# Another order of preparing v's tiles, five tiles of u ahead, and gathering that ends sooner, in a two-block kernel

## The chip, the cores and the metric

The kernel runs on one core of one Trainium2 chip. The metric is the device time of one execution in microseconds (us), as a median of runs. Five engines work side by side, each through its own instructions in the written order: TensorE (matrix products, with weight loads shown apart as PEld), VectorE (DVE), ScalarE (ACT), GpSimd (POOL, which here issues the indirect gathers) and SyncE (SP, which issues the other DMAs). Semaphores order them against each other.

## The reference

Two transformer blocks, one after the other, on 512 tokens of width 1024 in float32. Each block mixes tokens (the first by pooling and retention over a context, the second by HGRN2 and S5) and then runs a PEER layer: a product-key lookup chooses 16 of 16,384 experts for each token and each of 8 heads, and

    act = gelu(u[eidx] . h)            # one number per chosen expert
    out = sum(gate * act * v[eidx])    # rows of v, width 1024

where `u` and `v` are tables of 16,384 rows of 1024 numbers. The change touches only this PEER layer, which runs twice.

## The kernel before

Tokens come in four groups of 128. For three groups (`ND` = 3, 384 tokens, `TD`) the PEER layer is computed **densely**: all 16,384 experts are gone through in 128 tiles of 128 experts. A *tile of u* gives gelu(u.h) of 128 experts for 384 tokens; multiplied with a table of gates G (zero where an expert isn't chosen) this becomes the weights of a *tile of v*, whose products add up in six PSUM banks (`pv`). For the fourth group the chosen rows are **gathered** by indirect DMAs, 128 of u and 128 of v, 512 KB each, and are worked on by VectorE, one instruction per row (`sparse`, lines 2280, 2296, 2301). Each float32 operand is split into a high part in fp32r and the rest (`split`, lines 108 to 114), and each product is three matmuls (`mm3`, lines 118 to 120).

The first `L0` = 60 tiles of u are done earlier, while the gates are being computed, and their activations are parked in DRAM (*old* tiles, `Go` and `old` are their gates and activations, loaded four tiles at a time). The remaining 68 are done in `steady`, together with all 128 tiles of v and the gathering. `steady` is where the change lies:

- `LEAD` tiles of u are done first, with the loads of v's first two tiles issued after the first of them; then the first tile of v is prepared.
- A loop of 124 passes follows. Pass i issues the loads of v's tile i+2 on SP, does a tile of u where the schedule `s_by` asks for one (none after pass `S_END` = 112), calls `side`, prepares v's tile i+1 (`v_prep`) and issues the matmuls of v's tile i. Tiles of u call `side` once more. Tiles 124 to 127 of v are prepared on the way in other buffers and multiplied at the end.
- `side` owes gathered rows at a steady pace: 256/`full` rows per call, times `VF` after pass 112. When all 256 are consumed, it goes on with the finishing steps of the fourth group (`done`, `take`, `update`, `squares`, `factor`, lines 2312 to 2366), one per call; the first of them loads a row of gates from DRAM and uses it in the same call.
- `order` says which tile of v comes in which pass: a new one if its activation was made long enough ago, an old one otherwise.

`v_prep` turns a loaded tile of v (`raw`, named `vr`) into `vh` and `vl`, multiplies the activations with the gates (line 2255, in place), and splits the product into `wh` and `wl`. ScalarE writes the high parts, VectorE the rest. A tile of v can be multiplied once `wh` and `vh` are there; `vl` and `wl` are needed by the second and third matmul of a group. `vh`, `vl`, `wh`, `wl` have two buffers, `vr` three, a gathered row five, the gelu'd activation of a new tile six. A tile of u has one PSUM bank (`p0`), so the next tile of u waits until gelu has read it. Nothing is reordered by a scheduler: each engine works in the order in which the Python code issues.

Of the kernel before, what the change touches and what calls it, by code (L numbers as in the profile page):

```python
# [10 lines left out]
F32 = mybir.dt.float32  # L11
# [4 lines left out]
AF = mybir.ActivationFunctionType  # L16
ALU = mybir.AluOpType
# [11 lines left out]
class Env:  # L29
# [6 lines left out]
    def __init__(self, tc):  # L36
        self.tc, self.nc = tc, tc.nc
        self.now = 0
        self.queue = []
        self.chains = []  # L40
        self.fill, self.rate, self.owed = None, 0.0, 0.0
# [66 lines left out]
def split(nc, src, hi, lo, e_hi="act", e_lo="dve"):  # L108

    if e_hi == "act":  # L110
        nc.scalar.activation(hi, src, AF.Copy)  # L111
    else:
        (nc.vector if e_hi == "dve" else nc.gpsimd).tensor_copy(hi, src)
    (nc.vector if e_lo == "dve" else nc.gpsimd).tensor_tensor(lo, src, hi.bitcast(F32), op=ALU.subtract)  # L114
# [1611 lines left out]
class Peer:  # L1726
# [5 lines left out]
    LAG = 4  # L1732
    NQ, NT = 42, 8
    L0 = 60
    LEAD = 2
    S_END = 112
    RATE, RATE_T = 1.3, 1.3
    QT = 2
    WLO = "dve"
    SPARSE_END = 122  # L1740
    VF = 0.5

    def __init__(self, E, pfx, wq, key_rows, u, uT, v, AB, done, fill):
        self.E, self.pfx = E, pfx
        self.tc, self.nc = E.tc, E.nc
        self.wq, self.key_rows, self.u, self.uT, self.v = wq, key_rows, u, uT, v
        self.AB, self.done, self.fill, self.after = AB, done, fill, None
        self.TD = self.ND * 128
        self.few = sum(r.shape[1] for r in key_rows) <= 8
        self.U, self.V, self.Gt, self.act_tiles, self.old = {}, {}, {}, {}, {}  # L1750

        n = 128 - self.L0
        self.s_by = [min(n, self.LEAD + (i + 1) * (n - self.LEAD) // self.S_END) for i in range(128)]
        self.order, new, old = [], self.L0, 0
        for i in range(128):
            have = self.s_by[i - 1 - self.LEAD] if i > self.LEAD else 0
            if old == self.L0 or (new - self.L0 < have and i < 124):
                self.order.append(new)
                new += 1
            else:  # L1760
                self.order.append(old)
                old += 1
        assert sorted(self.order) == list(range(128)) and self.order[124] // self.GE == self.order[127] // self.GE
# [344 lines left out]
    def steady(self, vp, psv):  # L2108
# [5 lines left out]
        done = 0  # L2114
        for _ in range(self.LEAD):
            self.s_step(self.L0 + done)
# [7 lines left out]
        owed = 0.0  # L2124
        full = self.s_by[-1] - self.LEAD + self.S_END + self.VF * (self.SPARSE_END - self.S_END)
        finish = None
# [21 lines left out]
        def side():  # L2148
            nonlocal owed
            owed += 256 / full * (1.0 if i < self.S_END else self.VF)  # L2150
            while owed >= 1 and finish is None:
# [87 lines left out]
    def v_prep(self, e, vp, spare=False):  # L2239
        if e >= 128:  # L2240
            return
        nc = self.nc
        raw, G = self.V[e]
        if spare:
            vh, vl = (self.sp.tile([128, 8, 128], F32R, name=n).rearrange("p a b -> p (a b)") for n in ("uh", "ul"))
            p, n, b = (self.fp, "hs", 1) if e == 124 else (self.sp, "ur", 3)
            w2 = p.tile([128, 1024], F32R, name=n, bufs=b)
            wh, wl = (w2[:, i * self.TD:(i + 1) * self.TD] for i in range(2))
        else:
            vh, vl = (vp.tile([128, 1024], F32R, name=n, bufs=2) for n in ("vh", "vl"))  # L2250
            wh, wl = (vp.tile([128, self.TD], F32R, name=n, bufs=2) for n in ("wh", "wl"))
        split(nc, raw, vh, vl, "act", "dve")
        act = self.act_tiles.pop(self.order[e])
        a3 = act.rearrange("p (c t) -> p c t", t=self.TB)
        nc.vector.tensor_tensor(a3, a3, G, op=ALU.mult)  # L2255
        split(nc, act, wh, wl)
        self.V[e] = (wh, wl, vh, vl)

    def v_mm(self, es):
# [170 lines left out]
```

## Time and profile before

| | |
|---|---|
| median of 3 runs | 3644.05 us (3637.18 to 3645.54) |
| profiled execution, its own time | 3638.08 us |
| its span on the core | 3636.3 us |
| mean granted TensorE clock | 0.973 |
| TensorE busy | 3406.6 us (94%) |
| VectorE busy | 2829.1 us (78%) |
| ScalarE busy | 1380.6 us (38%) |
| GpSimd busy | 1117.7 us (31%) |
| DMA | 830.20 MB, mean 228 GB/s |

`steady` runs from about 1108 to 1962 us in the first block and from about 2771 to 3628 us in the second. A row of a timeline gives the start and the duration in us, the engine, the line, the operation, what it writes and reads, and in brackets how long the engine stood idle before and what ended that. PEld rows tell best when TensorE starts on something, since ends of matmuls are modelled.

### The profile page before, as it was taken

To read this page: it belongs to the slowest core of one execution; us is meant where nothing else is said; L and a number is where in the kernel's file an instruction comes from. 1 tells how busy PE (TensorE), PEld (TensorE's weight loads), DVE (VectorE), ACT (ScalarE), POOL (GpSimd) and SP (SyncE) were. 2 spreads that over 40 slices of the span, in tenths; PEclk is the share of its full clock that TensorE was granted. 3 is DMA by queue.
4 is the path that set the end of the run, shared out by engine and by line. 5 is a ranking of instruction groups with operands and counts; after the bars stand their busy time and mean duration, and the time that the engine had idled before them with its cause. 6 is when DMAs were issued, how large, how long until landed. Compare 5 with 4: busy or idle time off the path is not lost. (4 is left out here: it accounts for less than half of the span.)

```text
span 3636.3 us, 50853 instructions
## 1 busy us (share of the span) xinstructions
PE 3406.6 (94%) x18339; PEld 2992.4 (82%) x18339; DVE 2829.1 (78%) x6079; ACT 1380.6 (38%) x1930; POOL 1117.7 (31%) x1076
## 2 busy tenths in 40 slices
PE   8989887999998999999998888999998999999998
PEld 5878676999887888888886778899887888888886
DVE  6654743898996888888877685788996888888886
ACT  4223333332673333333334324432574333333333
POOL 3212675000003444444431432000001445444451
PEclk9999998999999999999998989999999999999999
DMA  5442754443459999999993213244457999999995
GB/s 189 137 148 71 217 172 104 131 135 126 176 201 327 359 345 352 339 338 348 329 322 115 70 57 103 95 141 139 143 206 269 341 373 325 350 341 336 348 323 193
DMA packets 418747, 830.20 MB, mean 228 GB/s; under 512 B 37948, under 2 KB 249776, under 8 KB 415424
## 3 DMA queue, kind: packets, MB, share of 16 engines
q1 hardware_dynamic: 344320, 558.41, 45.3%
q0 software_dynamic: 74176, 268.55, 20.3%
q8 instruction: 144, 2.36, 0.3%
q14 instruction: 107, 0.88, 0.1%
HBM read 744.52 MB, written 82.33 MB: 227 GB/s over the span
## 5 line engine op out<-in xcount | busy, mean ns | idle before, releaser
L2280 POOL DMA_INDIRECT gr<-in_peer_u_dram,rb x256 | 367.9, 1437 | 1406.5 <-DMA ur<-in_peer_u_tiles_dram 491.1
L118 PE MATMUL pv<-vh,wh 128*128 128x512 f32 x1512 | 602.3, 398 | 48.6 <-ACT wh L111 48.1
L120 PE MATMUL pv<-vh,wl 128*128 128x512 f32 x1512 | 604.3, 400 | 0.0
L119 PE MATMUL pv<-vl,wh 128*128 128x512 f32 x1512 | 594.6, 393 | 0.0
L2280 POOL DMA_INDIRECT gr<-in_peer_v_dram,rb x256 | 371.6, 1452 | 405.3 <-DVE accs L2301 343.0
L114 DVE TENSOR_TENSOR ul<-ur,uh 128x1024 fp32r<-128x1024 f32 x260 | 318.0, 1223 | 128.2 <-ACT uh L111 126.5
L118 PEld LDWEIGHTS pv<-vh,wh 128*128 128x128 f32 x1512 | 286.5, 189 | 126.7 <-ACT wh L111 75.2
L114 DVE TENSOR_TENSOR vl<-vr,vh 128x1024 fp32r<-128x1024 f32 x252 | 308.1, 1223 | 79.2 <-ACT vh L111 77.3
L118 PE MATMUL p<-hi,uh 128*128 128x384 f32 x1088 | 365.6, 336 | 1.4 <-ACT act L2074 1.4
L120 PE MATMUL p<-hi,ul 128*128 128x384 f32 x1088 | 365.7, 336 | 0.3 <-DVE ul L114 0.3
L119 PE MATMUL p<-lo,uh 128*128 128x384 f32 x1088 | 365.3, 336 | 0.0
L120 PEld LDWEIGHTS pv<-vh,wl 128*128 128x128 f32 x1512 | 286.1, 189 | 86.8 <-DVE wl L114 29.3
L118 PE MATMUL mm<-hi,uh 128*128 128x384 f32 x960 | 333.9, 348 | 3.6 <-ACT qT L1832 3.6
L119 PEld LDWEIGHTS pv<-vl,wh 128*128 128x128 f32 x1512 | 286.9, 190 | 52.6
L2301 DVE SCALAR_TENSOR_TENSOR accs<-gr,rb,accs 128x1024 f32<-128x1024 f32 x254 | 325.7, 1282 | 5.5 <-DMA gr<-in_peer_v_dram,rb 0.7
L120 PE MATMUL mm<-hi,ul 128*128 128x384 f32 x960 | 324.2, 338 | 4.5 <-DVE ul L114 4.5
L119 PE MATMUL mm<-lo,uh 128*128 128x384 f32 x960 | 323.0, 337 | 0.0
L2296 DVE SCALAR_TENSOR_TENSOR gr<-gr,hs 128x1024 f32<-128x1024 f32 x256 | 303.2, 1219 | 0.0
L111 ACT ACTIVATE vh<-vr 128x1024 fp32r<-128x1024 f32 x252 | 265.9, 1055 | 60.1 <-PE pv L120 30.8
L111 ACT ACTIVATE uh<-ur 128x1024 fp32r<-128x1024 f32 x260 | 272.6, 1048 | 5.5 <-DMA ur<-in_peer_u_tiles_dram 5.5
L118 PE MATMUL mm<-hi,whi 128*128 128x512 f32 (+1 forms) x656 | 262.3, 400 | 1.1 <-ACT hi L311 1.1
L120 PE MATMUL mm<-hi,wlo 128*128 128x512 f32 (+1 forms) x656 | 252.7, 385 | 1.3 <-DVE wlo L114 1.3
(625 smaller groups left out, 7079.5 us busy)
## 6 DMA issues: line engine op xcount, KB each, us to landing
ur<-in_peer_u_tiles_dram SPq DMA_DIRECT2D x256, 512.0 KB
vr<-in_peer_v_dram SPq DMA_DIRECT2D x252, 512.0 KB
raw<-in_w_in_dram SPq DMA_DIRECT2D x60, 512.0 KB
ada<-in_ada_w_dram SPq DMA_DIRECT2D x96, 256.0 KB
fG<-gst SPq DMA_DIRECT2D x12, 2048.0 KB
f_2G<-gst SPq DMA_DIRECT2D x12, 2048.0 KB
x<-in_ada_w_dram SPq DMA_DIRECT2D x64, 256.0 KB
raw<-in_peer_wq_dram SPq DMA_DIRECT2D x32, 512.0 KB
```

The costliest lines, as they stand in the source:

```text
L111: nc.scalar.activation(hi, src, AF.Copy)
L114: (nc.vector if e_lo == "dve" else nc.gpsimd).tensor_tensor(lo, src, hi.bitcast(F32), op=ALU.subtract)
L118: nc.tensor.matmul(out, a_hi, b_hi, start=start, stop=False)
L119: nc.tensor.matmul(out, a_hi, b_lo, start=False, stop=False)
L120: nc.tensor.matmul(out, a_lo, b_hi, start=False, stop=stop)
L2280: nc.gpsimd.indirect_dma_start(out=r, out_offset=None, in_=self.u if n < 128 else self.v, in_offset=bass.IndirectOffsetOnAxis(ap=self.eidx ...
L2296: nc.vector.scalar_tensor_tensor(r, r, 1.0, self.hs, op0=ALU.mult, op1=ALU.mult, accum_out=dots[:, j:j + 1])
L2301: nc.vector.scalar_tensor_tensor(accs, r, w[:, j:j + 1], accs, op0=ALU.mult, op1=ALU.add)
```

## The change

`v_prep` issues its five instructions in another order: the product with the gates first, then both high parts on ScalarE, then both low parts on VectorE. `LEAD` goes from 2 to 5; what `order` used of `LEAD` (how long ago an activation must have been made) becomes a constant of its own, `WAIT` = 2, the value it had. `SPARSE_END`, the pass by which the pace of gathering is set, goes from 122 to 118, and `VF` from 0.5 to 0.6.

```diff
-    LEAD = 2
+    LEAD = 5
+    WAIT = 2
...
-    SPARSE_END = 122
-    VF = 0.5
+    SPARSE_END = 118
+    VF = 0.6
...
-            have = self.s_by[i - 1 - self.LEAD] if i > self.LEAD else 0
+            have = self.s_by[i - 1 - self.WAIT] if i > self.WAIT else 0
...
-        split(nc, raw, vh, vl, "act", "dve")
         act = self.act_tiles.pop(self.order[e])
         a3 = act.rearrange("p (c t) -> p c t", t=self.TB)
         nc.vector.tensor_tensor(a3, a3, G, op=ALU.mult)
-        split(nc, act, wh, wl)
+        nc.scalar.activation(vh, raw, AF.Copy)
+        nc.scalar.activation(wh, act, AF.Copy)
+        nc.vector.tensor_tensor(vl, raw, vh.bitcast(F32), op=ALU.subtract)
+        nc.vector.tensor_tensor(wl, act, wh.bitcast(F32), op=ALU.subtract)
```

## Rows read from the trace of the kernel before

**Rows 1.** Page, busy us of each engine, share of the span, instructions.
```profile
PE 3406.6 (94%) x18339; PEld 2992.4 (82%) x18339; DVE 2829.1 (78%) x6079; ACT 1380.6 (38%) x1930; POOL 1117.7 (31%) x1076
```
**Rows 2.** Stretches: us, busy of PE, PEld, DVE, ACT, POOL; clock, DMA share, GB/s.
```profile
1120.00:1125.00 5.00, 0.00 (x0) 0.00 (x0) 0.00 (x0) 0.29 (x1) 0.00 (x0) 0.52 1.02 405
...
1500.00:1600.00 100.00, 98.67 (x478) 85.54 (x477) 84.62 (x95) 34.26 (x47) 49.11 (x34) 1.00 0.95 341
...
2900.00:3000.00 100.00, 97.28 (x468) 83.59 (x467) 84.16 (x125) 34.11 (x46) 47.81 (x32) 1.00 0.99 363
```
**Rows 3.** Timeline of PEld, block one: first weight load of a tile each.
```profile
1389.77 0.19 PEld L118 LDWEIGHTS p<-hi,uh 128*128 128x128 f32 x1
...
1393.98 0.19 PEld L118 LDWEIGHTS pv<-vh,wh 128*128 128x128 f32 x1
...
1398.02 0.19 PEld L118 LDWEIGHTS p<-hi,uh 128*128 128x128 f32 x1
...
1519.85 0.19 PEld L118 LDWEIGHTS pv<-vh,wh 128*128 128x128 f32 x1 [0.20 <-ACT wh L111]
...
1886.70 0.19 PEld L118 LDWEIGHTS pv<-vh,wh 128*128 128x128 f32 x1
...
1890.78 0.19 PEld L118 LDWEIGHTS pv<-vh,wh 128*128 128x128 f32 x1
```
**Rows 4.** Waits of PEld, 1135 to 1885 us: total us, times, longest.
```profile
PEld pv L118 <- ACT wh L111: 16.4, 43, 1.3
```
**Rows 5.** Timeline of DVE and ACT ahead of the load at 1519.85.
```profile
1516.40 1.05 ACT L111 ACTIVATE vh<-vr 128x1024 fp32r<-128x1024 f32 x1
...
1517.49 1.23 DVE L114 TENSOR_TENSOR vl<-vr,vh 128x1024 fp32r<-128x1024 f32 x1 [0.63 <-ACT vh L111]
...
1518.63 0.55 DVE L2255 TENSOR_TENSOR act<-act,Gn 128x384 f32<-128x384 f32 x1
...
1519.27 0.53 ACT L111 ACTIVATE wh<-act 128x384 fp32r<-128x384 f32 x1 [1.82 <-DVE act L2255]
...
1519.83 0.56 DVE L114 TENSOR_TENSOR wl<-act,wh 128x384 fp32r<-128x384 f32 x1 [0.65 <-ACT wh L111]
```
**Rows 6.** Timeline of PEld, start of `steady` in block one.
```profile
1108.74 0.19 PEld L118 LDWEIGHTS p<-hi,uh 128*128 128x128 f32 x1
...
1113.82 0.19 PEld L118 LDWEIGHTS p<-hi,uh 128*128 128x128 f32 x1 [0.90 <-ACT act L2074]
...
1128.10 0.29 PEld L118 LDWEIGHTS pv<-vh,wh 128*128 128x128 f32 x1 [10.17 <-ACT wh L111]
...
1134.79 0.19 PEld L118 LDWEIGHTS p<-hi,uh 128*128 128x128 f32 x1
```
**Rows 7.** Timeline of PEld, block two: start of `steady`, and v's tile 113.
```profile
2776.88 0.19 PEld L118 LDWEIGHTS p<-hi,uh 128*128 128x128 f32 x1 [1.14 <-ACT act L2074]
...
2794.56 0.29 PEld L118 LDWEIGHTS pv<-vh,wh 128*128 128x128 f32 x1 [13.03 <-ACT wh L111]
...
2800.89 0.19 PEld L118 LDWEIGHTS p<-hi,uh 128*128 128x128 f32 x1
...
3553.93 0.19 PEld L118 LDWEIGHTS pv<-vh,wh 128*128 128x128 f32 x1
```
**Rows 8.** Timeline of ACT: the first tile of v in either block.
```profile
1124.71 1.06 ACT L111 ACTIVATE vh<-vr 128x1024 fp32r<-128x1024 f32 x1 [5.93 <-DMA vr<-in_peer_v_dram]
...
2791.17 1.06 ACT L111 ACTIVATE vh<-vr 128x1024 fp32r<-128x1024 f32 x1 [8.79 <-DMA vr<-in_peer_v_dram]
```
**Rows 9.** Ends of the stages: DVE, ACT, PEld timelines; tile `pv`, first and last start.
```profile
1911.02 0.56 DVE L114 TENSOR_TENSOR wl<-old,wh 128x384 fp32r<-128x384 f32 x1 [0.65 <-ACT wh L111]
...
1924.48 1.06 ACT L111 ACTIVATE vh<-vr 128x1024 fp32r<-128x1024 f32 x1 [2.31 <-DMA vr<-in_peer_v_dram]
...
1962.20 0.13 PEld L272 LDWEIGHTS p<-ident,frr 128*128 128x128 f32 x1
...
L120 PE MATMUL pv<-vh,wl x1512: 387/389/683, 1129.1 to 3627.6; 128*128 128x512 f32 x189
```

## The prediction

> **What bounds the kernel now.** I read the busy times first: TensorE is busy 94% of the span [rows 1]. So an edit on another engine pays only where TensorE waits for it. The change touches the two stretches in which `steady` runs, 1108 to 1962 and 2771 to 3628 us. There TensorE runs at full clock, VectorE is busy some 85 us of 100, and DMA carries 341 to 363 GB/s [rows 2]. A busy share doesn't show lost matmul time, because a matmul's end is modelled; the starts of the weight loads do. So I read the timeline of those next. A tile of u takes 1393.98 - 1389.77 = 4.21 us; a tile of v takes 4.04 us before a tile of u and 4.08 us before another tile of v [rows 3]. Whatever exceeds this is waiting, and it falls into three places.
>
> *The middle of each stage.* From 1134.79 (second weight-load group of u after the first tile of v, [rows 6]) to 1886.70 [rows 3] there are 66 tiles of u and 112 of v; 46 of these are followed by another v. Unhindered: 66 x 4.21 + 66 x 4.04 + 46 x 4.08 = 732.2 us, and 1.9 us for two short transposes of the filler. Measured 751.9, so 17.8 us are lost. In stage two, 2800.89 to 3553.93 [rows 7] is 753.0: 18.9 us lost. The waits name the cause: TensorE for `wh` of ScalarE, 43 times, up to 1.3 us [rows 4]. I then read one such wait on the other engines [rows 5]: `vh` starts at 1516.40 and `wh` ends at 1519.80, 3.4 us later, though the two conversions together take 1.6 us. ScalarE stands still, because `wh` needs the gated product, and that product is queued on VectorE behind `vl`, which itself needs `vh`. When no tile of u lies between two tiles of v, this chain and the free-buffer wait in front of it fill the 4.08 us of the running tile and some more (0.20 us here [rows 3]).
>
> *The start of each stage.* Two tiles of u, then TensorE waits 10.17 and 13.03 us for the first `wh` [rows 6, 7], because ScalarE has waited until 1124.71 and 2791.17 for the first tile of v to arrive [rows 8], with DMA at 405 GB/s [rows 2]. The first tile of v then takes 6.69 us, at a granted clock of about half.
>
> *The end of each stage.* From the start of v's tile 113, fifteen tiles unhindered are 61.2 us. They take 1962.20 - 1886.70 = 75.5 and 3627.6 - 3553.93 = 73.7 us [rows 3, 7, 9]: 14.3 and 12.5 us lost.
>
> **The change part by part.**
>
> *New order in `v_prep`.* Nothing is added: the same five instructions for each of the 256 tiles. The product goes to the front on VectorE, where it waits for nothing of ScalarE; `wh` follows `vh` directly. From the start of `vh`, `wh` is ready after 1.05 + 0.53 = 1.6 us instead of 3.4, `vl` after 1.05 + 1.23 = 2.3, `wl` after 2.8 (durations [rows 5]). The tightest case has `vh` start 0.35 us after the tile before last has left its buffer, so the first matmul's operands are there 2 us before TensorE wants them, and `vl` and `wl` 1.4 and 1 us before. VectorE also loses its stall ahead of `wl` (0.65 us here). A wait of up to 1.3 us fits into this slack. I take 90% of 17.8 + 18.9: **33 us** gained. Bounds: all of it, 36.7; and 15, if the denser gathering puts VectorE late as often as not.
>
> *Denser gathering.* `LEAD` and `VF` change the step of the pacing: `full` was 66 + 112 + 0.5 x 10 = 183 and becomes 63 + 112 + 0.6 x 6 = 178.6, so a call of `side` owes 256/178.6 = 1.433 rows instead of 1.399. A loop pass makes 1 + 63/112 calls instead of 1 + 66/112: 2.24 rows against 2.22. Almost no more work per pass, but the pass shrinks from 751.9/112 = 6.71 us to 4.04 + 0.02 + 0.5625 x 4.21 = 6.43. VectorE's 85% of the stretch [rows 2] includes operations of the same kinds; per pass it grows by 4% of itself at most, and stays under 90%. I cost it at nothing; its cover is the 2 us of slack above.
>
> *Five tiles of u first.* The three extra tiles leave the passes (12.6 us a stage) and go into the idle start. They share one PSUM bank, so each waits for its gelu: spacing 1113.82 - 1108.74 = 5.08 us [rows 6]. In stage one the fifth starts at 1129.1 if its load is there. That load stands on SP's queue behind v's first two tiles; the first arrived by 1124.71, the two 0.52 MB transfers behind it take 2.6 us at 405 GB/s, so 1127.3, plus 1.05 for `uh`: in time. It ends at 1133.3; gelu, `vh` and `wh` (0.5 + 1.05 + 0.5 and hand-overs, 2.3 us) put the first tile of v at 1135.6. It ends at 1139.7 at full clock, 1142.3 at the half clock it had; before it ended at 1134.79. Gain: 12.6 less 4.9 to 7.5; I take 6.5. In stage two the load arrives at 2791.2 + 2.6 = 2793.8, so the fifth tile starts at 2794.9, ends at 2799.1 to 2801.7; v ends at 2805.5 to 2810 instead of 2800.89. Gain 12.6 less 4.6 to 9: I take 5.5. Together **12 us**, bounds 0 (the load a further 6 us late in each stage, since later loads of u now wait for buffers ahead of v's third tile) and 20 (all idle time filled).
>
> *`SPARSE_END` 118.* Counting the owed rows, gathering finishes at pass 119 instead of 123. The last additions leave passes 119 to 122, but the finishing steps move up. In VectorE's order the first `take` and `update` now stand in pass 119 **ahead** of the preparation of v's tile 120, and they need the gate row, whose DMA SP issues behind the gates and activations of v's last group (which wait for `wl` of tile 119) and v's tiles 124 and 125. Before, the next load at that place was v's: `wl` of 119 ended at 1911.58, that load was there at 1924.48 [rows 9], 12.9 us. So VectorE stops for some 13 us, plus 1.4 for the gain row behind it, plus 2 until the next `wh`, in all 16 us from the end of `wl`; TensorE has one or two finished tiles (4 to 8 us) and waits 8 to 12 us, and 2.6 for the clock. Against that, the 14.3 and 12.5 us lost there now shrink: the preparations are shorter by 1.8 us each, and the finishing steps no longer stand behind the last preparation. I set the end of the stages at **0**, bounds 10 gained and 15 lost, for both stages together.
>
> **The sum.** 33 + 12 + 0 = 45 us. The profiled execution took 3638.08 us (span 3636.3), 6 under the median of 3644.05 of the runs shown, which lie from 3637.18 to 3645.54. 3638 - 45 = 3593, and 3599 counted from the median; I forecast 3596.
>
> **The rivals.**
>
> *DMA becomes the bound: slower.* A pass moves 0.52 MB for v, 0.29 for u, 1.17 for 2.24 gathered rows, 0.28 for gates and old activations: 2.27 MB. At 6.43 us that is 353 GB/s. For it: DMA is already 95 to 99% busy at 341 and 363 GB/s [rows 2]. Against it: the same queues carried 405 GB/s at the start [rows 2], and in the middle of a stage almost no wait ends on a DMA. If DMA sustains only the 340 GB/s of today's pass (2.28 MB in 6.71 us), the pass stays at 6.7 us, nothing is gained in the middle, and v's first tile ends later by 6 and 7 us: 3638 + 13 = 3651. It decides below 341 GB/s, where a pass lasts 6.66 us and the lost start is just paid.
>
> The Trainium skill, in "DMA: Bandwidth & Descriptors" (Where 436 GB/s comes from), says that transfers between HBM and SBUF are bound by a core's share of HBM, about 358 GB/s. By that figure a pass would need 6.34 us (an estimate), just under 6.43, with nothing left for the filler's loads in the first third; the trace's 405 GB/s disagrees with it as a ceiling, and I lower this rival's chance accordingly.
>
> *The waits only change their name.* TensorE waits for `vl` or `wl` instead of `wh`, since three rows gathered one after the other hold VectorE up in front of the preparation. Then half of the middle's gain comes and half the start's: 3638 - 16.5 - 6 = 3615, or 3618 between profile and median.
>
> *The finishing steps cost.* The stop on the gate row isn't paid by shorter preparations: 12 us lost in each stage, 3596 + 24 = 3620.
>
> *The order does nothing*, because ScalarE's conversions weren't what is late: against it stand 43 waits of its name [rows 4]. Under 2%, counted with the DMA rival's milder form.
>
> **How the numbers follow.** Forecast 0.66 (3580 to 3612 as its own range), waits renamed 0.15, finishing steps 0.11, DMA bound 0.08. Ranging from 3578 (nearly all waits gone, and the end gains) to 3630 leaves out DMA bound and the outer ends of the others. About 0.2%, 7 us, is what a measurement can tell from no change. Faster: 0.66 + 0.15 + 0.11 less a little for overlaps, 0.89; same 0.04; slower 0.07, all from DMA.
>
> **What would show it.** Right: between v's first tile and tile 113 the weight loads of v following v start 4.08 us apart, and TensorE's waits for `wh` in the middle fall from 16 us to a few; five tiles of u 5.1 us apart, then a gap near 2.5 us; on VectorE a stop of 8 us or more in front of the first `take`, with the gate row's DMA as its releaser. Wrong: waits in the middle that end on DMAs of `vr`, `ur` or `gr`; the fifth u tile starting after 2800 us, or the like in stage one; ends of stages that lose over 25 us each.

## The result and the profile after

The changed kernel takes 3596.59 us (median of 4 runs, 3594.71 to 3598.08) against 3641.76 us before (4 runs, 3637.18 to 3645.54): ratio 0.9876, 95% interval 0.9863 to 0.9888, so 45 us faster. The forecast was 3596 us. The total is right, but in part by luck: the start gave half of what was forecast, and the middle and the ends gave more, as the experiments show.

The profiled execution took 3594.71 us, with a span of 3592.6 us and a mean granted clock of 0.974. The busy times of the page answer to [rows 1]: TensorE's share stays at 94%, and the span is shorter.

```profile
PE 3379.7 (94%) x18339; PEld 3007.1 (84%) x18339; DVE 2806.9 (78%) x6079; ACT 1359.8 (38%) x1930; POOL 1055.7 (29%) x1076
```

The stretches (columns as in [rows 2]) show TensorE busy all the time in the middle of either stage, VectorE 87 to 88 us of 100, and DMA at 357 to 364 GB/s with a share of 0.99 to 1.00; the first row is the start of block one, at half clock.

```profile
1130.00:1135.00 5.00, 3.75 (x11) 3.37 (x12) 2.92 (x3) 2.15 (x3) 0.00 (x0) 0.50 0.39 112
...
1500.00:1600.00 100.00, 100.00 (x493) 89.17 (x492) 87.44 (x97) 33.63 (x48) 49.07 (x35) 1.00 1.00 357
2900.00:3000.00 100.00, 100.00 (x486) 87.77 (x485) 88.39 (x132) 34.92 (x49) 45.83 (x34) 1.00 0.99 364
```

**The middle.** TensorE's waits between 1150 and 1860 us have no row at all. Before, there were 43 waits for `wh` [rows 4] and, in the row behind them in the same view, 46 for `wl` (total us, times, longest):

```profile
PEld pv L120 <- DVE wl L114: 13.6, 46, 0.3
```

In block two, 2800 to 3510 us, the longest entry is this one. It stood there before as well, behind 15.1 us of waits for `wh`:

```profile
PEld pv L118 <- ACT act L2075: 1.7, 2, 0.9
```

The timeline of PEld (first weight load of a tile each) answers to [rows 3], with no idle time in front of any: a tile of u takes 4.21 us, a tile of v 4.04 behind a tile of u and 4.08 behind another tile of v. Behind it, the timeline of DVE and ACT shows a preparation in the new order, as [rows 5] does the old: the product ends before `vh` begins, `wh` follows `vh` at once, and `wl` is done 2.8 us after the start of `vh`.

```profile
1389.51 0.19 PEld L118 LDWEIGHTS p<-hi,uh 128*128 128x128 f32 x1
...
1393.72 0.19 PEld L118 LDWEIGHTS pv<-vh,wh 128*128 128x128 f32 x1
...
1397.76 0.19 PEld L118 LDWEIGHTS p<-hi,uh 128*128 128x128 f32 x1
...
1401.98 0.19 PEld L118 LDWEIGHTS pv<-vh,wh 128*128 128x128 f32 x1
...
1406.02 0.19 PEld L118 LDWEIGHTS pv<-vh,wh 128*128 128x128 f32 x1
...
1410.10 0.19 PEld L118 LDWEIGHTS p<-hi,uh 128*128 128x128 f32 x1
...
1516.68 0.55 DVE L2255 TENSOR_TENSOR act<-act,Gn 128x384 f32<-128x384 f32 x1
1517.91 1.05 ACT L2256 ACTIVATE vh<-vr 128x1024 fp32r<-128x1024 f32 x1
1518.86 0.52 ACT L2257 ACTIVATE wh<-act 128x384 fp32r<-128x384 f32 x1
1518.99 1.23 DVE L2258 TENSOR_TENSOR vl<-vr,vh 128x1024 fp32r<-128x1024 f32 x1 [1.76 <-ACT vh L2256]
1520.13 0.55 DVE L2259 TENSOR_TENSOR wl<-act,wh 128x384 fp32r<-128x384 f32 x1
```

**The start.** Timeline of PEld, ACT and SP in block one, against [rows 6]. Three tiles of u follow the first at 5.0 to 5.1 us each, but TensorE waits 4.26 us for the fifth, which then lasts 6.6 us instead of 4.2, at the granted clock of 0.50 shown above. ScalarE had waited 6.94 us for its load, which SP issued behind v's two; the conversion of that load stands on ScalarE in front of the fourth tile's gelu, which frees the PSUM bank.

```profile
1107.78 0.19 PEld L118 LDWEIGHTS p<-hi,uh 128*128 128x128 f32 x1
...
1122.88 0.19 PEld L118 LDWEIGHTS p<-hi,uh 128*128 128x128 f32 x1 [0.90 <-ACT act L2075]
1131.25 0.28 PEld L118 LDWEIGHTS p<-hi,uh 128*128 128x128 f32 x1 [4.26 <-ACT act L2075]
1140.15 0.19 PEld L118 LDWEIGHTS pv<-vh,wh 128*128 128x128 f32 x1 [2.25 <-ACT wh L2257]
...
1145.02 0.19 PEld L118 LDWEIGHTS p<-hi,uh 128*128 128x128 f32 x1
...
1129.77 1.06 ACT L111 ACTIVATE uh<-ur 128x1024 fp32r<-128x1024 f32 x1 [6.94 <-DMA ur<-in_peer_u_tiles_dram]
...
1111.08 1.73 SPq L2237 DMA_DIRECT2D vr<-in_peer_v_dram  x2
1112.91 7.47 SPq L2058 DMA_DIRECT2D ur<-in_peer_u_tiles_dram  x3
```

**The end.** Timeline of DVE, PEld and SP at v's tile 120 in both blocks; before, nothing like it stood there [rows 9]. VectorE's first `take` waits 14.15 and 8.27 us for the gate row, whose load SP issued only at 1895.45 in block one, and TensorE waits behind it.

```profile
1904.51 0.69 DVE L2330 TENSOR_TENSOR vr<-accs,gr 128x512 f32<-128x512 f32 x1 [14.15 <-DMA gr<-gate]
...
3544.35 0.69 DVE L2330 TENSOR_TENSOR vr<-accs,gr 128x512 f32<-128x512 f32 x1 [8.27 <-DMA gr<-gate]
...
1907.78 0.29 PEld L118 LDWEIGHTS pv<-vh,wh 128*128 128x128 f32 x1 [12.55 <-ACT wh L2257]
...
3547.62 0.29 PEld L118 LDWEIGHTS pv<-vh,wh 128*128 128x128 f32 x1 [6.67 <-ACT wh L2257]
...
1891.89 3.25 SPq L2237 DMA_DIRECT2D ur<-in_peer_v_dram  x2
1895.45 0.40 SPq L2318 DMA_DIRECT2D gr<-gate  x1
```

Every profile is reduced in the same way to what TensorE loses in the three places, in us, block one / block two. *Start*: from the first tile of u to the end of v's first tile, less 4.21 for each tile of u in front. *Middle*: what the stretch up to v's tile 113 takes over its tiles at 4.21, 4.04 and 4.08 and over 1.9 us for the filler's operations. *End*: from tile 113 to the last weight load, over 61.2. Each row is one profiled execution; the median beside it is of 4 to 11 runs. On the chips of the experiments the kernel before had medians of 3641.7 to 3644.8 us; every ratio below is to the kernel before on the same chip. The two kernels and all that was tried:

| kernel | start | middle | end | median us |
|---|---|---|---|---|
| before | 17.6 / 20.9 | 17.8 / 18.9 | 14.3 / 12.5 | 3641.8 |
| changed | 16.2 / 16.2 | 0.1 / 0.6 | 15.2 / 10.3 | 3596.6 |
| 1 order alone | 18.9 / 18.9 | 0.2 / 2.7 | 6.9 / 2.1 | 3587.7 |
| 2 five tiles alone | 19.2 / 19.3 | 19.7 / 20.1 | 16.2 / 12.7 | 3640.5 |
| 3 pace alone | 20.6 / 20.5 | 24.4 / 22.3 | 26.4 / 25.1 | 3666.1 |
| 4 changed, steps held back | 15.6 / 17.5 | 0.1 / 0.6 | 11.8 / 5.4 | 3587.0 |
| 5 changed, steps and row loads held back | 16.2 / 17.0 | 0.1 / 0.6 | 7.7 / 3.5 | 3581.5 |
| 6 changed, old pace | 16.3 / 16.4 | 0.1 / 0.6 | 5.7 / 0.9 | 3579.3 |
| 7 as 6, four tiles | 14.0 / 14.3 | 0.1 / 0.6 | 6.8 / 2.1 | 3578.7 |
| 8 as 6, v's loads later | 12.2 / 12.3 | 0.1 / 0.7 | 5.6 / 1.0 | 3573.6 |
| 9 as 8, v prepared ahead | 7.2 / 7.6 | 0.1 / 0.6 | 5.5 / 1.0 | 3560.4 |
| 10 as 9, weights in pass 123 | 7.2 / 7.2 | 0.1 / 0.6 | 7.8 / 1.0 | 3563.9 |
| 11 as 9, weights after the passes | 7.2 / 7.5 | 0.1 / 0.6 | 0.9 / 0.9 | 3558.6 |

Between before and changed the table gives 6.1 at the start, 36.0 in the middle and 1.3 at the end, 43.4 of the 43.7 us between the two spans. Outside these stretches executions differ by a few us: the profiled ones of 3 and 9 lie 5 and 6.5 us above their medians.

### The profile page after: what moved, and what is told of

The parts are those of the page before. It is cut to its first block, busy times and chain, and to the rows that moved or that the text cites. A ratio compares the mean times of both kernels' runs of the same rounds, so it can differ in the third digit from the quotient of the medians.

```text
span 3592.6 us, 50851 instructions
## 1 busy us (share of the span) xinstructions
PE 3379.7 (94%) x18339; PEld 3007.1 (84%) x18339; DVE 2806.9 (78%) x6079; ACT 1359.8 (38%) x1930; POOL 1055.7 (29%) x1076
## 4 chain that ended last, share of the span: by engine, by line
PE 72%; DVE 16%; POOL 3%; DMA 3%; issue 3%; ACT 2%; SPq 1%; DVEq 0%; ACTq 0%; POOLq 0%
PE pv L118 9%; PE pv L119 9%; PE pv L120 9%; PE mm L118 8%; PE mm L119 8%; PE mm L120 8%; DVE ga L2036 5%; PE p L118 5%; PE p L120 5%; PE p L119 5%; DVE gb L2032 3%; DMA ada<-in_ada_w_dram 1%; DVE ul L114 1%; DMA ur<-in_peer_u_tiles_dram 1%; PE ch L1913 1%
## 5 line engine op out<-in xcount | busy, mean ns | idle before, releaser
L2283 POOL DMA_INDIRECT gr<-in_peer_u_dram,rb x256 | 336.0, 1313 | 1419.9 <-DMA ur<-in_peer_u_tiles_dram 979.3
L118 PE MATMUL pv<-vh,wh 128*128 128x512 f32 x1512 | 591.4, 391 | 22.8 <-ACT wh L2257 22.8
L120 PE MATMUL pv<-vh,wl 128*128 128x512 f32 x1512 | 590.7, 391 | 0.0
L2283 POOL DMA_INDIRECT gr<-in_peer_v_dram,rb x256 | 343.6, 1342 | 390.9 <-DVE accs L2304 331.4
L118 PEld LDWEIGHTS pv<-vh,wh 128*128 128x128 f32 x1512 | 285.0, 188 | 81.5 <-ACT wh L2257 25.1
L2075 ACT ACTIVATE act<-p 128x384 f32<-128x384 f32 x136 | 66.9, 492 | 702.3 <-PE p L120 691.4
```

The source lines that it names most:

```text
L118: nc.tensor.matmul(out, a_hi, b_hi, start=start, stop=False)
L120: nc.tensor.matmul(out, a_lo, b_hi, start=False, stop=stop)
L2283: nc.gpsimd.indirect_dma_start(out=r, out_offset=None, in_=self.u if n < 128 else self.v, in_offset=bass.IndirectOffsetOnAxis(ap=self.eidx ...
```

## The experiments

**The three parts alone (1 to 3).** Each takes one hunk of the diff and leaves the others.

```diff
 order alone: v_prep as changed; LEAD, SPARSE_END, VF as before
 five tiles alone
-    LEAD = 2
+    LEAD = 5
+    WAIT = 2
...
-            have = self.s_by[i - 1 - self.LEAD] if i > self.LEAD else 0
+            have = self.s_by[i - 1 - self.WAIT] if i > self.WAIT else 0
 pace alone
-    SPARSE_END = 122
-    VF = 0.5
+    SPARSE_END = 118
+    VF = 0.6
```

> Only the new order in v_prep; LEAD 2, SPARSE_END 122 and VF 0.5 as before. My theory (the product queued behind vl is what makes wh late): TensorE's waits in the middle of both stages go, 17.8 + 18.9 us; the starts stay as they were; the ends keep their late finishing steps and lose 3 to 5 us less each. 3642 - 37 - 8 = 3597, between 3590 and 3605, so about as fast as the whole change. Rival (order and five tiles ahead only work together, since prepared tiles need activations made earlier): 3615 to 3630, with waits for wh left in the middle.

> Only LEAD 5 (WAIT 2), old order in v_prep, old pace. From the trace of the changed kernel the start gains 1.4 and 4.7 us. With the old order the passes without a tile of u are 49 instead of 46 per stage, each losing about 0.4 us: 2.4 us back. My theory: 3642 - 6 + 2 = 3638, between 3632 and 3643. Rival (what I forecast, 12 us at the start): 3630.

> Only SPARSE_END 118 and VF 0.6, old order, LEAD 2. My theory: the finishing steps come four passes earlier, VectorE stops on the gate row in front of the preparation of v's tile 120 (14.2 and 8.3 us in the changed kernel), and the old, longer preparations follow: slower by 4 to 14 us, 3646 to 3656. Rival (gathering that ends sooner frees VectorE and DMA for the end of the stage): faster by 3 us or more, under 3639.

Against 3642.1 us of before on the same chip: order alone 3587.74 us (ratio 0.9855, 0.9839 to 0.9870); five tiles alone 3640.52 (0.9997, 0.9988 to 1.0006); pace alone 3666.06 (1.0063, 1.0049 to 1.0077). The second is in its range; the first is faster than its range and the third slower. The order alone gains 54 us, more than the whole change, because it also takes 17.8 us out of the ends (14.3 to 6.9 and 12.5 to 2.1; the longest tile there goes from 9.1 to 6.2 us). Of TensorE's waits between 1150 and 1860 us one is left (total, times, longest):

```profile
PEld pv L120 <- DVE wl L2258: 0.3, 1, 0.3
```

The pace alone costs 24 us between the medians; the table shows most of its loss at the ends, where VectorE's stop on the gate row has the same form as in the changed kernel. Timeline of DVE, pace alone:

```profile
1934.90 0.69 DVE L2327 TENSOR_TENSOR vr<-accs,gr 128x512 f32<-128x512 f32 x1 [12.83 <-DMA gr<-gate]
...
3609.16 0.69 DVE L2327 TENSOR_TENSOR vr<-accs,gr 128x512 f32<-128x512 f32 x1 [10.13 <-DMA gr<-gate]
```

The five tiles alone gain nothing. TensorE's waits of 1150 to 1860 us stay as they were without the new order (first line: total, times, longest; compare [rows 4]), and the two starts lose 38.5 us together, exactly as before. In the old order the wait for v's first `wh`, behind the fifth tile of u, is 4.12 us (second line, timeline of PEld) instead of the 2.25 of the changed kernel:

```profile
PEld pv L118 <- ACT wh L111: 18.0, 45, 1.7
...
1143.26 0.19 PEld L118 LDWEIGHTS pv<-vh,wh 128*128 128x128 f32 x1 [4.12 <-ACT wh L111]
```

**What in the pace costs (4 to 6).** First the finishing steps are kept out of the passes before 122; then the loads of gate row and gain row as well; then the old pace is put back.

```diff
 4: in side()
-            if finish is not None:
+            if finish is not None and i >= self.HOLD:    # HOLD = 122
 5: in ending(), ahead of self.done(rows)
             yield from sps
+            while i < 122:
+                yield
 6:
-    SPARSE_END = 118
-    VF = 0.6
+    SPARSE_END = 122
+    VF = 0.5
```

> The changed kernel, but the finishing steps (take and what follows) begin in pass 122 at the earliest; gathering and the load of the gate row stay in pass 119. My theory: the stop on the gate row no longer stands in front of tile 120, the waits of 12.6 and 6.7 us and the slow clock behind them (1.7 and 2.5 us) go, some of it comes back as later finishing work: 3597 - 16 = 3581, between 3574 and 3588. Rival (in block one tile 120 itself comes late, behind 2 MB of preloaded weights, in both cases it is the load that TensorE waits for): 3591 to 3597, the wait only changing its releaser to the load of v.

> The changed kernel with the old pace of gathering (SPARSE_END 122, VF 0.5): the new order and the five tiles of u stay. Theory: the denser pace is what costs in the changed kernel (the stop on the gate row ahead of tile 120's preparation, late loads of v behind it); without it the end of the stages loses 7 and 2 us as with the order alone, and the start keeps the changed kernel's 16.2 us in each block against 18.9 with the order alone: 3587.7 - 2 x 2.7 = 3582 us (3577 to 3587). Rival: the five tiles of u cost what the pace seemed to cost (they shift the schedule of tiles of u, and with it the pass in which gathering ends): 3592 us or more.

> The changed kernel with its dense pace, but the whole of the finishing part, the loads of its gate row and gain row included, not before pass 122 (before, with only the steps held back and the two loads left in pass 119, the ends still lost 11.8 and 5.4 us). Theory: denser gathering itself costs nothing; its price is the finishing part moved up, half as VectorE's stop on the gate row, half because the two row loads stand on SP's queue in front of v's last tiles. Then the ends lose 5.7 and 0.9 us as with the old pace, and the time is that of the old pace, 3579 us (3575 to 3584). Rival: the denser gathering delays v's last tiles by itself (transfers collide): 3587 us as with the steps alone held back.

4 took 3587.04 us (ratio to before 0.9844, 0.9831 to 0.9858), inside the theory's range but at its slow end, and the rival's sign is there too. The stop on the gate row is gone, but SP still issues the two rows in pass 119, in front of v's last tiles, and ScalarE now waits for those, 8.40 us at the longest (in 6 the same wait is 4.63). Timeline of ACT and SP of 4, block one:

```profile
1910.91 1.06 ACT L2257 ACTIVATE vh<-vr 128x1024 fp32r<-128x1024 f32 x1 [8.40 <-DMA vr<-in_peer_v_dram]
...
1899.21 0.40 SPq L2319 DMA_DIRECT2D gr<-gate  x1
1899.66 0.42 SPq L2320 DMA_DIRECT2D lo<-in_final_g_dram  x1
1900.12 3.26 SPq L2238 DMA_DIRECT2D vr<-in_peer_v_dram  x3
```

6 took 3579.26 us (0.9829, 0.9815 to 0.9844), as the theory said: 17 us less than the changed kernel. Its ends lose 5.7 and 0.9 us instead of 15.2 and 10.3, and its middle exactly what the changed kernel's does. 5 took 3581.54 us (0.9824, 0.9810 to 0.9838), in its range: with the dense pace kept and the whole finishing part moved back, all but 4.6 us of the 18.9 that the pace adds at the ends is gone. So denser gathering by itself is nearly free; what it moves up isn't.

**What in the five tiles falls short (7 to 9).** All with the old pace.

```diff
 7:
-    LEAD = 5
+    LEAD = 4
 8 and 9, in steady():
-            if not done:
+            if done == 1:
                 self.v_load(0, vp)
                 self.v_load(1, vp)
 9 also: v_prep(0, vp) ahead of the last s_step, not behind it
         for _ in range(self.LEAD):
+            if done == self.LEAD - 1:
+                self.v_prep(0, vp)
             self.s_step(self.L0 + done)
```

> As the run with the old pace, but four tiles of u in front (LEAD 4) instead of five: those whose loads have landed when the stage begins. Theory: the fourth ends 19.4 us after the first began, wh is there 2.3 us later if v's first tile has landed (some 16 us after the first tile of u began in the kernel before), and v's first tile ends after 25.8 to 28.4 us: less 4 x 4.21 a start of 9 to 11.5 us instead of 16.2, so 3582 - 12 = 3570 us (3565 to 3576). Rival: the loads of u's next tiles in front of v's third, or v's first tile landing late, eat it: 3578 us or more.

> As the run with the old pace, and the loads of v's first two tiles are issued after the second tile of u, behind the load of u's fifth tile, no longer in front of it. Theory: the fifth tile of u stops for 4.3 us and then runs at half clock only because its load lands behind v's; with the load in front, it starts 5.1 us after the fourth, at full clock, and the start loses some 11 us in each block instead of 16.2: 3582 - 10 = 3572 us (3566 to 3577), with no wait of ScalarE for u's fifth tile. Rival: DMA carries all it can there, so v's first tile lands later by as much and TensorE stops in front of it: no difference to the run with the old pace, within 3 us.

> As the run with the old pace and the loads of v behind that of u's fifth tile, and v's first tile is prepared ahead of the fifth tile of u instead of behind it. Theory: the 2.8 us that TensorE still waits for v's first wh, and the slow clock in the tile behind it (6.2 to 6.5 us instead of 4.04), are the preparation's own chain, which the fifth tile of u hides when v's first tile has landed by then: the start loses some 8 us in each block instead of 12.2, so 3573.6 - 8 = 3565 us (3561 to 3570). Rival: v's first tile lands too late for that, VectorE and ScalarE stop in front of it and hold up the gelu or the next tile of u: 3573 us or more.

7 took 3578.67 us (0.9824, 0.9811 to 0.9838): no better than five tiles, against the theory. The starts lose 4.4 us less than those of 6, not some 12, and the ends 2.3 more. The same load of u is still in the way. The fifth tile's `uh` stands in front of the fourth tile's gelu and v's `vh` on ScalarE and waits for its load until 1127.20; TensorE stands 5.89 us. Timeline of ACT and PEld of 7:

```profile
1127.20 1.06 ACT L111 ACTIVATE uh<-ur 128x1024 fp32r<-128x1024 f32 x1 [6.66 <-DMA ur<-in_peer_u_tiles_dram]
...
1128.53 1.05 ACT L2256 ACTIVATE vh<-vr 128x1024 fp32r<-128x1024 f32 x1
...
1130.59 0.29 PEld L118 LDWEIGHTS pv<-vh,wh 128*128 128x128 f32 x1 [5.89 <-ACT wh L2257]
```

8 took 3573.56 us (0.9812, 0.9798 to 0.9825), 5.7 less than 6, in the range of the theory. The fifth tile starts 5.0 us after the fourth and runs at full clock; v's first tile still waits 2.82 us and takes 6.19. Timeline of PEld of 8:

```profile
1129.09 0.19 PEld L118 LDWEIGHTS p<-hi,uh 128*128 128x128 f32 x1 [0.90 <-ACT act L2075]
...
1136.03 0.19 PEld L118 LDWEIGHTS pv<-vh,wh 128*128 128x128 f32 x1 [2.82 <-ACT wh L2257]
...
1142.22 0.19 PEld L118 LDWEIGHTS p<-hi,uh 128*128 128x128 f32 x1
```

9 took 3560.43 us (0.9764, 0.9751 to 0.9777), a little under its range: v's tile lands at 1132.7, is ready before u's fifth tile ends, and takes 4.04 us with no wait. Of the 13 us between the medians of 8 and 9 the table shows 9.7 in the starts; where the rest lies is not shown. Timeline of ACT and PEld of 9:

```profile
1132.72 1.06 ACT L2257 ACTIVATE vh<-vr 128x1024 fp32r<-128x1024 f32 x1 [1.36 <-DMA vr<-in_peer_v_dram]
...
1131.41 0.19 PEld L118 LDWEIGHTS p<-hi,uh 128*128 128x128 f32 x1 [0.90 <-ACT act L2075]
...
1135.51 0.19 PEld L118 LDWEIGHTS pv<-vh,wh 128*128 128x128 f32 x1
...
1139.55 0.19 PEld L118 LDWEIGHTS p<-hi,uh 128*128 128x128 f32 x1
```

**What is left at the end of block one (10 and 11).** With the old pace block one still loses 5.6 us and block two 1. Only block one loads 2 MB of the next stage's weights in pass 117.

```diff
             if i == 117 and self.after is not None:
                 self.after.preload()
 10: the same two lines at i == 123, behind v's loads
 11: behind the loop over the passes and v_prep(127)
```

> As the run before it, and the 2 MB of the next stage's weights that SP issues in pass 117 of block one are issued in pass 123. Theory: block one's end loses 5.6 us and block two's 1.0 with the same order of work, because these 2 MB stand in front of v's tiles 119 to 122 in block one; without them the end of block one loses 1 to 2 us: 4 us less than the run before it, 3561 us (3557 to 3566). Rival: the loss is the late load of the old activations behind a busy queue, or the next stage now waits for its weights by as much: no difference within 2 us.

> As the run with v's first tile prepared ahead of u's fifth, and the 2 MB of the next stage's weights are issued after the last pass of block one, behind the gate row and the gain row, no longer in pass 117 (and not in pass 123, where they stood directly in front of the gate row and VectorE stopped 5.7 us on it). Theory: with nothing large in front of v's last tiles or of the gate row, block one's end loses about 1 us as block two's does, against 5.5: 3560.4 - 4.5 = 3556 us (3551 to 3561), every tile of v from 113 on at 4.08 us but one. Rival: the weights are then late for the next stage, which stops for them: 3560 us or more, with a wait of ScalarE or TensorE on the loads of hi after 1925 us.

10 took 3563.87 us (0.9776, 0.9763 to 0.9789). That is inside its range, but only because 9 came out some 5 us under its own forecast; against the theory, 10 isn't shown to be faster than 9, and the end of block one loses 7.8 us where 1 to 2 were expected. The tiles of v up to 123 run at 4.08 us without a gap, so the weights had been what delayed them; but in pass 123 they stand in front of the gate row, and VectorE stops there. Timeline of DVE and SP of 10:

```profile
1904.75 0.69 DVE L2331 TENSOR_TENSOR vr<-accs,gr 128x512 f32<-128x512 f32 x1 [5.70 <-DMA gr<-gate]
...
1892.82 2.06 SPq L152 DMA_DIRECT2D hi<-in_w_in_dram  x4
1895.18 1.05 SPq L2319 DMA_DIRECT2D gr<-gate  x1
```

11 took 3558.61 us (0.9768, 0.9754 to 0.9781). It is in its range. The end of block one loses 0.9 us, and no wait on the weights appears behind it. The profile confirms the 4.6 us; the medians of 9 and 11 differ by only 1.8, less than their runs scatter, so the total doesn't show it. (The profile of 9 is of the slowest of its five runs.) Whichever of the two is the faster, both lie about 85 us under the kernel before and about 37 under the changed one.

## Why the prediction was right, and where it was not

- **The new order, 33 us in the middle: right in mechanism and size.** 36.0 us by the table, nearly all of the 36.7 lost there, and 33.8 with the order alone. ScalarE's own work was unchanged; it had been waiting for VectorE's order of work. The text told the 4.04 and 4.08 us of a tile of v apart by the tile that follows; it is the tile in front (rows 1401.98 to 1410.10 above), which leaves the sum as it is. The step missed that the same shortening is worth another 17.8 us at the ends; the text counted it only as something that shrinks there.
- **Denser gathering at nothing: right for the middle.** The changed kernel and the one with the old pace lose the same 0.1 and 0.6 us. The named cover, 2 us of slack from the new order, agrees with the pace alone: without that order its middles lost 6.6 and 3.4 us more than before.
- **Five tiles of u, 12 us: the mis-sized term; it measured 6.1** (1.4 and 4.7, inside the bounds of 0 to 20), and it needs the new order: alone the five tiles gave nothing at the starts, and added to the order 5.1 us (37.8 lost with the order alone, 32.7 in 6). The chain of 2.3 us from the last tile of u to v's first was right for the new order (2.25) and is 4.12 in the old. The text put v's first tile at its end some 32.2 us after the first tile of u began in block one (12.6 less 6.5 on top of 26.05); it was 37.24. Of the 5.0 us, 3.1 are the fifth tile's later start (23.5 us after the first instead of 20.4), and 2.4 its half clock, which the sum charged in block one only to v's tile; v's tile was 0.5 shorter than the middle of its two cases. So the sign of five tiles 5.1 us apart failed at the fifth. In block two, where the late load was reckoned with, the fifth tile started 23.5 us after the first, as forecast (23.3). The late start comes from the step that let two transfers of 0.52 MB land in 2.6 us, as though the 405 GB/s of [rows 2] were SP's queue alone. The DMA view of the changed kernel, 1109 to 1131 us, shows that SP's queue (first line) had 68% of the engines' time and the gathered rows (second line) 31%:

```profile
q1 hardware_dynamic: 3005, 5.67, 68.2%
q0 software_dynamic: 720, 2.62, 30.8%
```

  SP's 5.67 MB in these 22 us are 258 GB/s; at that rate the two transfers take 4.1 us (an estimate), which accounts for 1.5 of the 3.1; the rest is open. That the load's place on the queue was what failed is shown by 8: with it in front of v's, the stop and the half clock are gone.
- **The end at 0: right as a sum, with both sides larger than thought.** The new order gives 17.8 us there (the ends of 6, with five tiles as well, lose 2.4 less still), and what the pace moved up takes 18.9 (15.2 and 10.3 against 5.7 and 0.9). That these sizes cancel is luck. The stop on the gate row was forecast at some 13 us and measured 14.15 and 8.27; TensorE's wait at 8 to 12 and 2.6 for the clock, and measured 12.55 and 6.67, with the tile behind taking 5.7 and 6.6 us instead of 4.08. The mechanism stood in the text; its consequence, that the change would be faster without this part, did not.
- **The total.** Against 33, 12 and 0 the table shows 36.0, 6.1 and 1.3: an error of -5.9 us stands against +3.0 and +1.3. That the forecast came out within a us is luck; that the middle carries it is not.
- **The rivals.** DMA does not bind: the middle carries 357 to 364 GB/s without a wait of TensorE on a transfer, a pass at 6.4 us, above the 341 from which that rival decided. The waits did not change their name. The finishing steps did cost, but the order paid for them.

The Trainium skill's "DMA: Bandwidth & Descriptors" (Where 436 GB/s comes from) has transfers between HBM and SBUF bound at about 358 GB/s a core. The middle's 357 to 364 GB/s at a share of 0.99 to 1.00 lie close to it, yet a stretch of the kernel before carried 405 GB/s [rows 2], so here it is no ceiling.

## What to carry to other kernels

When an engine waits for another in front of every tile, look whether the producer's queue holds an operation that needs nothing of the consumer behind one that does: swapping two instructions in VectorE's order gave 54 us of 3642. A parameter that makes a side stream end sooner also moves up what follows it; list the loads in that part, and what stands behind each on its queue, before calling it free. Judge the parts of a change singly, since here the best of them alone (3588 us) was faster than all three together (3597), where the pace took back 17.

## What was not expected of the hardware

In the changed kernel DMA held 357 to 364 GB/s over stretches of 100 us at a share of 0.99 to 1.00 while TensorE waited for no transfer; a full share here was no sign of a bound. And a stop of 4.26 us cost TensorE 2.4 us more behind it: the next tile of u ran at a granted clock of 0.50 (1.2 GHz) and took 6.6 us instead of 4.2.
